# Row-wise infinity norm on one core: joined reductions in the tail's whole loads, and the first tile's store issued at the end

## Chip, core and metric

The kernel runs on one core of a Trainium2 chip. The metric is the device time of one execution in microseconds, given as the median of several runs. The core has several engines that run side by side and meet through semaphores: here VectorE (DVE) computes, SyncE (SP) issues the loads and the last store, ScalarE (ACT) issues the other two stores, and GpSimd (POOL) closes the program. Transfers between the chip's main memory (HBM) and the on-chip memory (SBUF, 128 partitions) are carried by 16 DMA engines.

## What is computed

```python
def setup_inputs():
    rows = 8192
    cols = 8192
    return {"x": np.random.randn(rows, cols).astype(np.float32)}

def reference(x: np.ndarray) -> np.ndarray:
    return np.linalg.norm(x, ord=np.inf, axis=1)
```

With `axis=1` this is the vector norm of each row: the largest absolute value of its 8192 numbers. 268 MB go in and 32 KB come out.

## The kernel before

Each of the 128 partitions handles 64 rows, in three groups with a result tile each: 2 rows of the first tile (`r_first`), 38 rows of the bulk (`r_bulk`) and 24 rows of the tail (`r_tail`). The input is loaded into one SBUF buffer, `ring`, which has room for three loads of two rows (`W` = 16384 columns) and a little padding.

The first loop (lines 263 to 268) does `N` = 20 loads of two rows for each partition, going round the three slots of the ring. Each load is followed by one reduction with two results: VectorE reads 128x16384 as two rows and writes 128x2. The first of these loads gives `r_first`, the other 19 give `r_bulk`. The reduction is `absmax` (line 254), so all of VectorE's instructions have line 255 in the profile.

The tail (lines 271 to 318) covers the last 24 rows of each partition as one line of 196608 columns, cut into the 37 loads of the list `TAIL`. Its first three entries are whole loads of 16384 columns that begin at a row's start; the later ones shrink from 15488 columns to 512, so that little work is left when the last one lands. A load that crosses a row's end is cut into pieces, one for each row. A piece that does not end its row gives a partial result, which is written into `ring` just in front of the place where the row's last piece will lie; the row's last piece is reduced together with these partial results, and gives the row's value in `r_tail`. The pieces of a load are separate VectorE instructions with one result each, in the whole loads too: each of these three gives two instructions of 128x8192, for two rows.

The places of the tail's loads in the ring follow from a small planner (lines 282 to 293): each load is put behind the one before it, rounded up to 128 columns with room for its partial results, and at the start of the ring again where it would run over the end. A load may only be written to where earlier reductions have read their data, so SyncE's issue of a load waits for VectorE. The tile framework makes these waits out of the reads and writes of the program; it also gives each DMA one of eight semaphores in turn, in the order of the DMAs in its schedule, and a DMA that gets a semaphore waits for the one that had it before, where that isn't implied already. Instructions of one engine run in the order in which they are issued.

The results leave in three stores. `r_bulk`'s and `r_first`'s are issued on ScalarE (lines 315 and 317), `r_tail`'s on SyncE (line 318). `r_bulk`'s has an explicit order behind the reduction of the third load from the end (`done`, line 316). `r_first`'s has none: it waits only for the first tile's reduction, and in ScalarE's program it stands ahead of `r_bulk`'s store.

Four passes work on the finished program. `drop_implied_waits` (line 134) takes out waits that other waits imply. `start_first_load_early` (line 34) puts the first load ahead of the opening barrier. `finish_on_pool` (line 71) lets GpSimd close the program alone: after the closing barrier it waits for the stores that nothing has waited for yet, clears the semaphores except the one of the last store (`r_tail`'s), and then waits for that one. `open_without_vector` (line 184) keeps VectorE out of the opening barrier.

Of the kernel before, what the change touches and what calls it, by code (L numbers as in the profile page):

```python
# [210 lines left out]
@with_exitstack  # L211
def kernel(
    ctx: ExitStack,
    tc: tile.TileContext,
    x: bass.AP,
    out: bass.AP,
    B: int = 2,
    SLOTS: int = 3,
    PAD: int = 128,
):  # L220
    nc = tc.nc
    P = nc.NUM_PARTITIONS
    rows, cols = x.shape
    W = B * cols
    R = SLOTS * W + PAD * 4


    n_tail = sum(w for _, w in TAIL) // cols
    met = 0
    for lo, w in sorted(TAIL):  # L230
        assert lo == met
        met += w
    assert met == n_tail * cols
    n_bulk_rows = rows // P - n_tail
    assert n_bulk_rows % B == 0
    N = n_bulk_rows // B
    split = n_bulk_rows * P
    x_f = x[: P * B].rearrange("(p b) c -> p (b c)", p=P)
    out_f = out[: P * B].rearrange("(p b) -> p b", p=P)
    x_b = x[P * B : split].rearrange("(p n b) c -> n p (b c)", p=P, b=B)  # L240
    out_b = out[P * B : split].rearrange("(p n) -> p n", p=P)
    x_t = x[split:].rearrange("(p t) c -> p (t c)", p=P)
    out_t = out[split:].rearrange("(p t) -> p t", p=P)

    pool = ctx.enter_context(tc.tile_pool(name="sbuf", bufs=1))
    r_first = pool.tile([P, B], F32)
    r_bulk = pool.tile([P, n_bulk_rows - B], F32)
    r_tail = pool.tile([P, n_tail], F32)
    used = [HEAD, B, n_bulk_rows - B, n_tail]
    gap = -sum(-(-n // STEP) * STEP for n in used) % PAD  # L250
    pool.tile([P, gap], F32, name="gap")
    ring = pool.tile([P, R], F32)

    def absmax(o, i):
        return nc.vector.reduce_max(  # L255
            out=o, in_=i, axis=X, apply_absolute_value=True
        )

    def after(ins, first, kind):
        info = mybir.DependencyInfo(kind, mybir.DependencyReason.SCHED_ONLY)  # L260
        tc.add_manual_dep(ins.ins, first.ins.name, info, reason="order")

    for n in range(N):
        at = n % SLOTS * W
        t = ring[:, at : at + W]
        nc.sync.dma_start(out=t, in_=x_f if n == 0 else x_b[n - 1])
        r = r_first[:] if n == 0 else r_bulk[:, (n - 1) * B : n * B]
        absmax(r, t.rearrange("p (b c) -> p b c", b=B))


    pieces = []
    for j, (at, w) in enumerate(TAIL):
        end = at + w
        while at < end:
            r = at // cols
            to = min(end, (r + 1) * cols)
            pieces.append((j, r, to - at))
            at = to
    of_row = [[k for k, s in enumerate(pieces) if s[1] == r] for r in range(n_tail)]


    here = N % SLOTS * W
    start, slot = [], []
    for j, (_, w) in enumerate(TAIL):
        first = next(s for s in pieces if s[0] == j)
        ks = of_row[first[1]]
        n_part = len(ks) - 1 if pieces[ks[-1]][0] == j else 0
        at = -(-(here + n_part) // PAD) * PAD
        if at + w > R:
            at = -(-n_part // PAD) * PAD  # L290
        start.append(at)
        slot.append(at - n_part)
        here = at + w

    for j, (src, w) in enumerate(TAIL):
        at = start[j]
        nc.sync.dma_start(out=ring[:, at : at + w], in_=x_t[:, src : src + w])
        here = [k for k, s in enumerate(pieces) if s[0] == j]
        offs = [at + sum(pieces[i][2] for i in here[:m]) for m in range(len(here))]
        todo = list(zip(here, offs))  # L300
        if slot[j] != at:

            todo = todo[1:] + todo[:1]
        for k, lo in todo:
            _, r, n = pieces[k]
            ks = of_row[r]
            if k == ks[-1]:
                frm = slot[j] if len(ks) > 1 else lo
                done = absmax(r_tail[:, r : r + 1], ring[:, frm : lo + n])
            else:  # L310
                to = slot[pieces[ks[-1]][0]] + ks.index(k)
                done = absmax(ring[:, to : to + 1], ring[:, lo : lo + n])
        if j == len(TAIL) - 3:

            ins = nc.scalar.dma_start(out=out_b, in_=r_bulk[:])
            after(ins, done, mybir.DependencyClass.Sync)
            nc.scalar.dma_start(out=out_f, in_=r_first[:])
    nc.sync.dma_start(out=out_t, in_=r_tail[:])
    nc.at_finalize(drop_implied_waits)
    nc.at_finalize(start_first_load_early)  # L320
    nc.at_finalize(finish_on_pool)
    nc.at_finalize(open_without_vector)
# [30 lines left out]
```

## Time and profile before

| what | value |
|---|---|
| median of 3 runs | 626.75 us (626.57 to 626.91) |
| the profiled execution | 626.98 us |
| its span (first to last instruction recorded) | 624.33 us |
| time outside the span | 2.65 us |
| one load of two rows, issue to landing | 40.7 us (median of 23) |
| `r_first`'s store, issue to landing | 23.5 us |
| `r_bulk`'s store, issue to landing | 1.5 us |
| `r_tail`'s store, issue to landing | 1.4 us |

How to read it: the page gives each engine's busy time and share of the span, then the DMA queues with packets, megabytes and share of 16 engines' time. In the rows of the timeline stand start and duration in us, the engine (with a q for its DMA issues), the line, the operation, the tile written and the tile read, their shapes, and how many instructions were merged; in brackets the engine's idle time just before, and what ended it. In the list of waits stand who waited, for whom, the us in total, the number of times and the longest. In the rows of groups stand the busy us and the mean ns of one, then the idle time before them. Consecutive VectorE instructions overlap a little in the records (by about 0.08 us), so durations do not add up exactly to distances between starts.

### The profile page before, as it was taken

Reading aid. Unit: us, or ns where it says so; the run is one execution under the profiler, and the core shown is the slowest. Engines: PE = TensorE matmul, PEld = TensorE weight load, DVE = VectorE, ACT = ScalarE, POOL = GpSimd, SP = SyncE. Lnnn points to the kernel's source line nnn. Section 1 sums busy time; section 2 is a strip of 40 time slices with the busy share of each in tenths; the row PEclk is TensorE's granted clock in tenths of the full one; section 3 lists DMA queues with packets and bytes.
Section 4 is the critical chain, followed back from the end, with each engine's and each line's share of the span. In section 5 each row is a group of like instructions: output and inputs, shape, how many; then the busy total and the mean of one; then the engine's idle time right before and its main releaser. Section 6 shows DMA issues by size and latency. Waiting matters only on the chain.

```text
span 624.3 us, 168 instructions
## 1 busy us (share of the span) xinstructions
DVE 553.2 (89%) x76; POOL 0.2 (0%) x4
## 2 busy tenths in 40 slices
DVE  0588988889988889888898888988899999999999
POOL 0000000000000000000000000000000000000000
DMA  9999999999999999999999999999999999999998
GB/s 403 470 403 458 416 428 445 403 470 403 470 403 470 403 466 407 458 416 428 445 403 470 403 470 403 470 403 470 392 435 458 408 446 427 421 437 424 431 425 335
DMA packets 8497, 268.47 MB, mean 430 GB/s; under 512 B 1200, under 2 KB 1200, under 8 KB 3120
## 3 DMA queue, kind: packets, MB, share of 16 engines
q1 hardware_dynamic: 8208, 268.44, 99.6%
q10 hardware_dynamic: 288, 0.02, 0.0%
q14 instruction: 1, 0.01, 0.0%
HBM read 268.44 MB, written 0.03 MB: 430 GB/s over the span
## 4 chain that ended last, share of the span: by engine, by line
DMA 61%; DVE 38%; issue 0%; DVEq 0%
DMA ring<-in_x_dram 61%; DVE r_bulk L255 17%; DVE ring L255 10%; DVE r_tail L255 9%; DVE r_first L255 3%; DVEq L348 0%
## 5 line engine op out<-in xcount | busy, mean ns | idle before, releaser
L255 DVE TENSOR_REDUCE r_bulk<-ring 128x2 f32<-128x16384 f32 x19 | 327.2, 17220 | 40.0 <-DMA ring<-in_x_dram 40.0
L255 DVE TENSOR_REDUCE r_tail<-ring 128x1 f32<-128x8192 f32 (+14 forms) x24 | 109.6, 4585 | 7.7 <-DMA ring<-in_x_dram 7.7
L255 DVE TENSOR_REDUCE ring<-ring 128x1 f32<-128x5248 f32 (+26 forms) x32 | 101.4, 3213 | 0.8 <-DMA ring<-in_x_dram 0.8
L255 DVE TENSOR_REDUCE r_first<-ring 128x2 f32<-128x16384 f32 x1 | 17.2, 17219 | 21.9 <-DMA ring<-in_x_dram 21.9
L337 POOL MEMSET const-bfloat16-1.0<- 128x1 bf16 x1 | 0.1, 101 | 0.0
L337 POOL MEMSET const-uint8-127<- 128x1 uint8 x1 | 0.1, 101 | 0.0
L337 POOL MEMSET const-float32-0.0<- 128x1 f32 x1 | 0.1, 98 | 0.2 <-issue 0.2
L337 POOL MEMSET const-float32-1.0<- 128x1 f32 x1 | 0.1, 98 | 0.0
## 6 DMA issues: line engine op xcount, KB each, us to landing
ring<-in_x_dram SPq DMA_DIRECT2D x1, 7744.0 KB, 39.6
ring<-in_x_dram SPq DMA_DIRECT2D x1, 7168.0 KB, 37.2
ring<-in_x_dram SPq DMA_DIRECT2D x1, 6400.0 KB, 32.9
ring<-in_x_dram SPq DMA_DIRECT2D x1, 5696.0 KB, 36.7
ring<-in_x_dram SPq DMA_DIRECT2D x1, 5056.0 KB, 41.0
ring<-in_x_dram SPq DMA_DIRECT2D x1, 4544.0 KB, 36.0
ring<-in_x_dram SPq DMA_DIRECT2D x1, 4032.0 KB, 32.0
ring<-in_x_dram SPq DMA_DIRECT2D x1, 3648.0 KB, 40.3
```

Of the source, the lines that this page charges most:

```text
L255: return nc.vector.reduce_max(out=o, in_=i, axis=X, apply_absolute_value=True)
L337: nc = _bacc.Bacc("TRN2", target_bir_lowering=False, num_devices=1)
```

## The change

The three whole loads of the tail get one reduction each, with two results, in the form that the bulk uses; they leave the loop body before the cutting into pieces. `r_first`'s store gets the same explicit order as `r_bulk`'s, behind the reduction of the third load from the end, and so stands behind `r_bulk`'s store in ScalarE's program.

```diff
     for j, (src, w) in enumerate(TAIL):
         at = start[j]
         nc.sync.dma_start(out=ring[:, at : at + w], in_=x_t[:, src : src + w])
+        if w == W and src % cols == 0:
+            r = src // cols
+            absmax(
+                r_tail[:, r : r + B],
+                ring[:, at : at + w].rearrange("p (b c) -> p b c", b=B),
+            )
+            continue
         here = [k for k, s in enumerate(pieces) if s[0] == j]
...
             ins = nc.scalar.dma_start(out=out_b, in_=r_bulk[:])
             after(ins, done, mybir.DependencyClass.Sync)
-            nc.scalar.dma_start(out=out_f, in_=r_first[:])
+            ins = nc.scalar.dma_start(out=out_f, in_=r_first[:])
+            after(ins, done, mybir.DependencyClass.Sync)
     nc.sync.dma_start(out=out_t, in_=r_tail[:])
```

In the built program VectorE has 73 reductions instead of 76. The eight DMA semaphores are handed out in another order, since `r_first`'s store no longer takes the third turn; each load still follows the load eight places before it on its semaphore. SyncE has one separate semaphore wait fewer (it stood at the ninth bulk load, for `r_first`'s store), and GpSimd has one more, for `r_first`'s store, ahead of its clearing of semaphores.

## The prediction

> **What bounds the kernel now.** I read the page from its DMA part first, since the kernel reads 268 MB and does one reduction on it.
>
> ```profile
> span 624.3 us, 168 instructions
> DVE 553.2 (89%) x76; POOL 0.2 (0%) x4
> q1 hardware_dynamic: 8208, 268.44, 99.6%
> q10 hardware_dynamic: 288, 0.02, 0.0%
> q14 instruction: 1, 0.01, 0.0%
> ```
>
> q1 is SyncE's queue, the loads: it keeps the 16 DMA engines busy for 99.6% of the span. VectorE works 89% of it. So the loads set the pace, and VectorE has slack, unless it lies in the wrong place. q10 is ScalarE's queue, which carries two of the three stores; q14 carried one packet of instructions. Both matter below. Next, who waited for whom:
>
> ```profile
> DVE r_bulk L255 <- DMA ring<-in_x_dram: 40.0, 19, 2.2
> DVE r_tail L255 <- DMA ring<-in_x_dram: 7.7, 5, 2.1
> DVE ring L255 <- DMA ring<-in_x_dram: 0.8, 1, 0.8
> ```
>
> VectorE waits some 2.1 us for every load of the bulk (40.0/19), in the tail five times (7.7 in all), and once more for 0.8 us. The timeline says where:
>
> ```profile
> 406.32 58.35 SPq L297 DMA_DIRECT2D ring<-in_x_dram  x4
> 408.36 17.28 DVE L255 TENSOR_REDUCE r_tail<-ring 128x1 f32<-128x8192 f32 x2 [2.07 <-DMA ring<-in_x_dram]
> 427.66 17.28 DVE L255 TENSOR_REDUCE r_tail<-ring 128x1 f32<-128x8192 f32 x2 [2.02 <-DMA ring<-in_x_dram]
> 447.04 17.28 DVE L255 TENSOR_REDUCE r_tail<-ring 128x1 f32<-128x8192 f32 x2 [2.10 <-DMA ring<-in_x_dram]
> 465.29 8.69 DVE L255 TENSOR_REDUCE r_tail<-ring 128x1 f32<-128x8192 f32 x1 [0.98 <-DMA ring<-in_x_dram]
> ...
> 573.24 0.33 SPq L297 DMA_DIRECT2D ring<-in_x_dram  x1
> 573.25 5.62 DVE L255 TENSOR_REDUCE ring<-ring 128x1 f32<-128x5248 f32 x1 [0.80 <-DMA ring<-in_x_dram]
> ```
>
> The three pairs are the instructions that the change joins; before and behind each VectorE waits for data. The last wait ends at 573.25; from there to 623.56 VectorE never waits. But it is not far behind the data: the semaphore events of the trace say that each later load lands 0.11 to 0.25 us before VectorE starts on it (0.024 us is the distance where it does wait). So the end is set by two things that run side by side with 0.1 to 0.2 us between them.
>
> **Part 1: one instruction instead of two, three times.** A pair takes 17.28 us from first start to last end. The joined form stands in the bulk, same shape:
>
> ```profile
> L255 DVE TENSOR_REDUCE r_bulk<-ring 128x2 f32<-128x16384 f32 x19 | 327.2, 17220 | 40.0 <-DMA ring<-in_x_dram 40.0
> ```
>
> 17.22 us, so 0.06 saved each, 0.18 in all. Behind the three pairs stand waits of 2.02, 2.10 and 0.98 us for data, so VectorE only waits 0.06 longer. What could pass on is the release of the slots: SyncE issues the next load just after the second half is done (425.64 to 425.67, 444.94 to 444.97, 464.31 to 464.34), and would now do so 0.06 earlier. A load lands 40.7 us after issue and takes 19.3 of DMA time, so about two are always queued ahead; an issue 0.06 earlier lands nothing earlier. The danger is the other sign: a load that needs only the first half of a slot could start after the first instruction today and would have to wait 8.6 us longer. I laid the ring out by the planner's rule: loads 3 and 4 of the tail (counted from 0) cover both halves of loads 0 and 1, and load 5 covers the end of load 1 and both halves of load 2. No load is freed by a first half alone. Bounds: -0.18 (no cover at all) to 0; I take 0.
>
> **Part 2: the early store goes.** Its 128 pieces of 8 bytes run between load packets from 42.8 to 62.4 us.
>
> ```profile
> 39.16 0.38 ACTq L317 DMA_DIRECT2D out_dram<-r_first  x1
> 41.21 17.22 DVE L255 TENSOR_REDUCE r_bulk<-ring 128x2 f32<-128x16384 f32 x1 [2.08 <-DMA ring<-in_x_dram]
> 60.65 17.22 DVE L255 TENSOR_REDUCE r_bulk<-ring 128x2 f32<-128x16384 f32 x1 [2.22 <-DMA ring<-in_x_dram]
> ```
>
> The wait grows from 2.08 to 2.22 there. A single interval varies anyway (19.27 to 19.38 elsewhere, in a pattern of four loads), so I compare four loads: 77.34 us from 41.21 to 118.55, against 77.30, 77.28 and 77.28 for the next three fours. The store cost the loads 0.04 to 0.06 us; by its packets, 9 for each engine at 9 ns, it would be 0.08. I take 0.06 saved. It passes to the end, because every later landing moves, the one at 573.2 included. Bounds: 0.04 to 0.08.
>
> **Part 3: the same store at the end.**
>
> ```profile
> 622.28 1.28 DVE L255 TENSOR_REDUCE r_tail<-ring 128x1 f32<-128x519 f32 x2
> 622.39 0.34 ACTq L315 DMA_DIRECT2D out_dram<-r_bulk  x1
> 623.59 0.35 SPq L318 DMA_DIRECT2D out_dram<-r_tail  x1
> ```
>
> ScalarE issues r_bulk's store at 622.39; its packets run from 623.24 to 623.47 and it lands at 623.85, 1.45 after issue. r_first's is queued right behind: issue at about 622.75, packets from 623.6 to about 623.8, landing at about 624.2. Its other waits (a landed load, the same reduction) are over by then. ScalarE would reach the closing barrier at about 623.3 instead of 622.9; SyncE reaches it at 624.1, so that is covered. r_tail's store is issued at 623.59, has packets from 624.4 and lands at 625.03: behind r_first's, and not beside it. GpSimd, which ends the program, leaves the barrier at 624.24 and waits for the ScalarE stores, clears semaphores, then waits for r_tail's. It gets one more wait, some 0.08 us (its barrier steps stand at 624.15 and 624.22), under the 0.8 us until 625.03. ScalarE's first DMA took 379 ns to issue and the second 338, so r_bulk's may be 0.04 late; hidden too. I take 0. Upper bound: if the two ScalarE stores ran strictly one behind the other, r_first's would land at 623.85 + 1.45 = 625.30, 0.27 behind the store that now ends last, and GpSimd's clearing, which now has 0.79 us of cover (624.24 to 625.03), would come after it: 0.27 + 0.79 + 0.08 = +1.14. Lower bound 0.
>
> The Trainium skill (DMA: Bandwidth & Descriptors, Anatomy of one DMA) gives a fixed cost of about 2.0 us for a DMA, most of it the receipt from memory. It is stated for another queue; by it r_first's store would land at 624.75, after the barrier, and if all of that counted the end would be 0.5 us later. The trace shows 1.45 for the neighbouring store.
>
> **Part 4: the instruction packet.** The page's one q14 packet is 8192 bytes, and lies at 570.37 to 570.68 us. The load that VectorE waits for at 573.25 took 7.16 us after the one before it, for 5248 columns, while 16384 columns take 19.31, so 6.19 for this one: 0.97 late. Until then the 16 parts of a load land within 0.5 us of each other; from then to the end within 1.3 to 1.4. So one DMA engine fell some 0.9 us behind and never caught up, and the end waits for it. I read it as an engine's program being fetched on as it runs. VectorE started its 48th reduction at 568.97, SyncE issued its last load before that at 566.13; 1.4 us from VectorE's step fits the 0.8 to 1.0 us from issue to first packet of other DMAs better. With three instructions fewer VectorE reaches that place in its program at 583.2, three reductions on; SyncE (one separate semaphore wait fewer) would reach it at 573.2. Either way the engine still falls behind, only later: VectorE starts the load of 573.25 up to 0.80 earlier, gets ahead, and then waits for the late engine. What is gained at the end is the smallest distance left between landing and start: 0.111 - 0.024 = 0.09 us if the packet falls before the next load lands (578.7), 0.163 - 0.024 = 0.14 if at 585. I take 0.12. Bounds: 0 (it doesn't move) to 0.80 (it no longer hurts).
>
> The Trainium skill (Runtime: NRT & Kernel Launch, Instruction fetch mechanics) says that crossing a block boundary of the program is mostly hidden. By that rule this part gives nothing, and the sum would be 626.7; here the engine that carried the packet was late by 0.97 us on the row that ended VectorE's wait.
>
> **Sum.** 0 - 0.06 + 0 - 0.12 = -0.18 us. The profiled execution took 626.98 (span 624.33 and 2.65 around it), so it would take 626.80. It was 0.23 above the median of 626.75, to which I apply the same difference: 626.57, say 626.6.
>
> **Rivals.** *The late engine is spared*: the packet moves to where it costs nothing. For: an engine that is ahead could carry it, as parts land 0.5 us apart. Against: lag has stayed for 50 us, and VectorE's program must still be read. Price: the 0.80 wait and the 0.06, so 625.9. *The closing store decides (slower)*: r_first's store lands late and GpSimd starts its clearing after it. Place: GpSimd after 624.24; it decides when the landing comes after that by more than the slack under 625.03, which the trace doesn't show. For: my landing of 624.2 is almost at the barrier. Against: packets of 9 to 14 ns, and both earlier stores landed within 1.5 us. Price 0.08 to 1.14 less 0.06, the middle 627.3. *Only the early store counts*: the packet doesn't move, or not with these instructions: 626.7.
>
> **Chances.** Forecast 0.50, only the early store 0.20, late engine spared 0.12, closing store 0.15, something unseen 0.03. The range 625.8 to 627.2 holds the first three and half of the fourth, about 9 in 10 by these cases; I leave it there because the bounds of parts 3 and 4 reach these ends. The likeliest case's own range is 626.4 to 626.75. By 0.2%, or 1.25 us, which is about what a measurement of this kernel can tell from no change, none of the priced cases differs. What is left outside are errors of my reading: a larger lag moved by the packet on the one side, the closing sequence on the other: faster 0.07, same 0.87, slower 0.06.
>
> **What would show it.** Part 1: waits of about 2.1 and 1.0 behind three reductions of 17.22. Part 2: no larger wait at 60.6. Part 3: two ScalarE issues after 622, landing before r_tail's store. Part 4: the 0.80 at 573 gone, a wait of up to 0.9 some loads later, and q14's packet near it. It is wrong if VectorE waits longer than before at any load before 573, if the DMA rate of the bulk changes, or if the time around the span is no longer 2.65.

## The result, and the profile after

The changed kernel takes 628.18 us (median of 16 runs, 627.75 to 628.72) against 626.87 for the kernel before (16 runs, 626.57 to 627.47): a ratio of 1.0019, 95% interval 1.0012 to 1.0026. It is 1.31 us slower, where 0.2 us faster was forecast. The profiled execution took 628.36 us.

The page first, its header and the rows of engines and of SyncE's queue:

```profile
span 624.3 us, 164 instructions
DVE 553.0 (89%) x73; POOL 0.2 (0%) x4
q1 hardware_dynamic: 8208, 268.44, 99.7%
```

The span is what it was, 624.3 us. So the loss lies outside the span: 628.36 - 624.31 = 4.05 us here, 2.65 before. Over the 16 runs the time outside is 4.1 us (median), and the span's median 624.0; for the kernel before, 33 later runs give 2.64 and 624.2. The change took about 0.2 us off the span and added 1.47 behind it.

What happens behind the span is seen in the DMA records. The timeline of the end, then the stores' rows in the table of DMA issues (queue, number, size, us from issue to last landing):

```profile
622.27 1.28 DVE L255 TENSOR_REDUCE r_tail<-ring 128x1 f32<-128x519 f32 x2
622.38 0.37 ACTq L322 DMA_DIRECT2D out_dram<-r_bulk  x1
622.79 0.44 ACTq L324 DMA_DIRECT2D out_dram<-r_first  x1
623.58 0.35 SPq L326 DMA_DIRECT2D out_dram<-r_tail  x1
```

```profile
out_dram<-r_bulk ACTq DMA_DIRECT2D x1, 19.0 KB, 1.7
out_dram<-r_first ACTq DMA_DIRECT2D x1, 1.0 KB, 3.3
out_dram<-r_tail SPq DMA_DIRECT2D x1, 12.0 KB, 2.8
```

Before, the last of these rows read:

```profile
out_dram<-r_tail SPq DMA_DIRECT2D x1, 12.0 KB, 1.4
```

The issues stand where they were expected. The smallest store, 1 KB, takes the longest: 3.3 us. The store behind it, `r_tail`'s, is issued at the same moment as before (623.58 against 623.59) and lands after 2.8 us where it took 1.4. The store ahead of it on the same queue, `r_bulk`'s, is a little late too: 1.7 us where it took 1.5. By the semaphore events the 16 parts of `r_first`'s store land between 624.14 and 626.05, one part after another, although all its packets had left by 623.94. Of `r_tail`'s 16 parts six land by 624.93, as before, and the other ten up to 626.41. Before, the last one landed at 625.03. The time of the execution is the last landing, counted from the span's start, plus 626.98 - 625.03 = 1.95 us before and 628.36 - 626.41 = 1.95 after (any time ahead of the span's start is in the 1.95): the later landing is the whole loss.

The joined reductions stand as forecast, with the same waits behind them:

```profile
408.77 17.22 DVE L255 TENSOR_REDUCE r_tail<-ring 128x2 f32<-128x16384 f32 x1 [2.09 <-DMA ring<-in_x_dram]
428.05 17.22 DVE L255 TENSOR_REDUCE r_tail<-ring 128x2 f32<-128x16384 f32 x1 [2.06 <-DMA ring<-in_x_dram]
447.37 17.22 DVE L255 TENSOR_REDUCE r_tail<-ring 128x2 f32<-128x16384 f32 x1 [2.10 <-DMA ring<-in_x_dram]
465.68 8.69 DVE L255 TENSOR_REDUCE r_tail<-ring 128x1 f32<-128x8192 f32 x1 [1.09 <-DMA ring<-in_x_dram]
```

And the instruction packet has moved from 570.37 to 581.72 us: in the window from 581 to 583 us the queue rows show it, and the timeline shows the wait of 0.80 us at 573 gone and one of 0.38 at 583.65:

```profile
572.75 10.07 DVE L255 TENSOR_REDUCE ring<-ring 128x1 f32<-128x5248 f32 x2
...
583.65 0.28 DVE L255 TENSOR_REDUCE ring<-ring 128x1 f32<-128x128 f32 x1 [0.38 <-DMA ring<-in_x_dram]
```

```profile
q14 instruction: 1, 0.01, 1.0%
```

### The profile page after: what moved, and what is told of

Read it like the earlier page. It is cut to its first block, busy times and chain, and to the rows that moved or that the text cites. A ratio compares the mean times of both kernels' runs of the same rounds, so it can differ in the third digit from the quotient of the medians.

```text
span 624.3 us, 164 instructions
## 1 busy us (share of the span) xinstructions
DVE 553.0 (89%) x73; POOL 0.2 (0%) x4
## 4 chain that ended last, share of the span: by engine, by line
DMA 62%; DVE 38%; issue 0%; DVEq 0%
DMA ring<-in_x_dram 62%; DVE r_bulk L255 17%; DVE ring L255 9%; DVE r_tail L255 9%; DVE r_first L255 3%; DVEq L356 0%
## 5 line engine op out<-in xcount | busy, mean ns | idle before, releaser
L255 DVE TENSOR_REDUCE r_tail<-ring 128x2 f32<-128x16384 f32 (+15 forms) x21 | 109.4, 5218 | 7.9 <-DMA ring<-in_x_dram 7.9
```

The lines of the kernel that those rows point to most:

```text
L255: return nc.vector.reduce_max(out=o, in_=i, axis=X, apply_absolute_value=True)
```

## The experiments

In each, "outside" is the time of a run less its span. All diffs are against the changed kernel unless another is named; they show the lines that matter, and `...` marks what is left out. The time that a result is set against is the kernel before's, run beside it. Experiments 7 to 11 are single executions, without an interval.

**1. The joined reductions alone.**

```diff
-            ins = nc.scalar.dma_start(out=out_f, in_=r_first[:])
-            after(ins, done, mybir.DependencyClass.Sync)
+            nc.scalar.dma_start(out=out_f, in_=r_first[:])
```

> Only the joined reductions; r_first's store stays early. Theory A (the store at the end costs the time: its 8-byte pieces are acknowledged late and hold back r_tail's landing): r_tail's store lands about 1.4 us after issue as before, the time outside the span is 2.65 us as before, and the time is 0 to 0.3 us under the kernel before (the instruction packet moves from 570 to about 582 us and the wait of 0.80 us shrinks). Rival B (the joined reductions cost the time, by some wait at the end that the records don't show): 1.1 to 1.4 us above the kernel before, about 628.2.

Measured: 626.85 us (11 runs) against 626.90, ratio 0.9995 (0.9987 to 1.0004), outside 2.64 for both. `r_tail`'s store lands 1.4 us after issue, with the same row as in the kernel before. The joined reductions cost nothing at the end.

**2. The moved store alone** (against the kernel before).

```diff
-            nc.scalar.dma_start(out=out_f, in_=r_first[:])
+            ins = nc.scalar.dma_start(out=out_f, in_=r_first[:])
+            after(ins, done, mybir.DependencyClass.Sync)
```

> Only the store is moved; VectorE keeps 76 reductions. Theory A: r_first's store lands more than 3 us after issue, r_tail's about 2.8 us after issue, the time is 1.2 to 1.6 us above the kernel before. Rival B: no slower than the kernel before. Beside it, for the instruction packet: if VectorE's place in its program sets it off, it stays at 570.4 us with the wait of about 0.8 us at 573; if SyncE's does (one separate wait fewer), it moves to 574 to 578 us.

Measured: 628.11 us (11 runs) against 626.90, ratio 1.0019 (1.0010 to 1.0028), outside 4.07 (median).

```profile
out_dram<-r_first ACTq DMA_DIRECT2D x1, 1.0 KB, 2.8
out_dram<-r_tail SPq DMA_DIRECT2D x1, 12.0 KB, 2.5
```

That is a little under what was written for them. `r_bulk`'s store, ahead of them, took 1.9 us. The store alone makes the whole loss. This kernel also says who sets off the instruction packet. The timeline, and the queue rows of the window from 569.5 to 571.5 us:

```profile
573.20 5.62 DVE L255 TENSOR_REDUCE ring<-ring 128x1 f32<-128x5248 f32 x1 [0.61 <-DMA ring<-in_x_dram]
```

```profile
q14 instruction: 1, 0.01, 1.0%
```

With 76 reductions and SyncE's shorter program it stays at 570.3 us, while in the first experiment, with 73 reductions and SyncE's program as before, it stands at 581.75. It goes with VectorE's program. In all fourteen traces it comes 3.4 to 4.2 us after VectorE starts its 47th reduction, whichever reduction that is.

**3. No store of `r_first` at all.**

```diff
...
-    x_b = x[P * B : split].rearrange("(p n b) c -> n p (b c)", p=P, b=B)
-    out_b = out[P * B : split].rearrange("(p n) -> p n", p=P)
+    x_b = x[:split].rearrange("(p n b) c -> n p (b c)", p=P, b=B)
+    out_b = out[:split].rearrange("(p n) -> p n", p=P)
...
-            ins = nc.scalar.dma_start(out=out_f, in_=r_first[:])
-            after(ins, done, mybir.DependencyClass.Sync)
```

> The first tile's rows become part of the bulk, 40 rows for each partition, and their results leave with r_bulk's store in pieces of 160 bytes; there is no store of r_first at all. Joined reductions as in the changed kernel. Theory A: r_tail's store lands about 1.4 us after issue, 2.65 us outside the span, time 0.1 to 0.4 us under the kernel before, so about 626.6. Rival C (what costs is that ScalarE's queue has no early DMA any more, or that the semaphores are handed out in another order): about 628, like the changed kernel. The rows of a load lie 40 rows apart in memory here and not 38, which could change the loads' rate; the landings of the bulk tell (19.3 us for each).

Measured: 626.61 us (11 runs) against 626.90, ratio 0.9996 (0.9987 to 1.0005), outside 2.64, loads of the bulk 19.3 us each. ScalarE's queue has no early DMA here, and the loads' semaphores go round as in the changed kernel: neither shows a cost.

**4. The same small pieces, spread out.** The loads are those of the third experiment, and `r_first` keeps its own store at the end.

```diff
...
+    out_all = out[:split].rearrange("(p n) -> p n", p=P)
+    out_f, out_b = out_all[:, :B], out_all[:, B:]
...
```

> Both stores at the end as in the changed kernel, but the first tile's two rows are the first of each partition's 40, so that r_first's 128 pieces of 8 bytes go to places 160 bytes apart and not to one stretch of 1 KB. Theory A1 (many small pieces into the same few memory lines are written one after another): r_first's store lands within 1.7 us, r_tail's after about 1.4, the time is that of the kernel with one store, about 626.7. Theory A2 (a piece of 8 bytes costs some 15 ns at the memory wherever it goes): r_first's lands 3.3 us after issue as in the changed kernel, and the time is about 628.2.

Measured: 626.51 us (11 runs) against 626.90, ratio 0.9995 (0.9986 to 1.0004), outside 2.64. The stores' rows:

```profile
out_dram<-r_bulk ACTq DMA_DIRECT2D x1, 19.0 KB, 1.5
out_dram<-r_first ACTq DMA_DIRECT2D x1, 1.0 KB, 1.5
out_dram<-r_tail SPq DMA_DIRECT2D x1, 12.0 KB, 1.4
```

The same 128 pieces of 8 bytes, at the same place in the program, from the same queue: 1.5 us. It is not the small piece, but where its neighbours lie.

**5. The moved store some 12 us earlier, while loads still run.**

```diff
+        if j == len(TAIL) - 14:
+            ins = nc.scalar.dma_start(out=out_f, in_=r_first[:])
+            after(ins, done, mybir.DependencyClass.Sync)
         if j == len(TAIL) - 3:
...
-            ins = nc.scalar.dma_start(out=out_f, in_=r_first[:])
-            after(ins, done, mybir.DependencyClass.Sync)
```

> The changed kernel, but r_first's store is ordered behind the reduction of the 14th load from the end, so it is issued at about 610.7 us, some 12 us ahead of r_tail's store; where it goes is as in the changed kernel. Theory A (pieces of 8 bytes into one KB are taken slowly, and what is stored right behind them waits): 2.64 us outside the span as in the kernel before, time 626.5 to 626.9. Rival (any store of r_first that is late in ScalarE's program costs the time): 628.1.

Measured: 628.28 us (11 runs) against 627.06, ratio 1.0015 (1.0007 to 1.0024), outside 2.68, but the span's median is 625.6 where the kernel before has 624.4. I was right on what lies outside and wrong on the time; the rival's 628.1 comes close, but its loss lies inside the span. The timeline around the store, and SyncE's waits after 600 us:

```profile
610.33 0.38 ACTq L321 DMA_DIRECT2D out_dram<-r_first  x1
615.72 1.35 DVE L255 TENSOR_REDUCE ring<-ring 128x1 f32<-128x1152 f32 x1 [0.85 <-DMA ring<-in_x_dram]
617.34 3.07 DVE L255 TENSOR_REDUCE ring<-ring 128x1 f32<-128x1024 f32 x3 [0.27 <-DMA ring<-in_x_dram]
```

```profile
SPq L297 <- DMA out_dram<-r_first: 5.5, 1, 5.5
```

The pieces leave between 613.8 and 615.2, and the two loads that land around them come late: VectorE waits 0.85 and 0.27 us where the changed kernel shows no wait, together 1.1 us, about the loss. What leaves beside or behind the slow pieces comes late, loads as well as stores. SyncE is also held for 5.5 us, since a load has to wait for the store whose semaphore it takes over; the loads were late before that wait ended at 617.6.

**6. The two ScalarE stores in the other order.**

> The changed kernel with the two ScalarE stores in the other order, r_first's ahead of r_bulk's, both behind the same reduction. Theory A: r_first's store starts 0.4 us earlier, so r_tail's lands some 0.4 us earlier than in the changed kernel, and the time outside the span falls from 4.1 to about 3.7; r_bulk's store, now behind it, lands over 2 us after issue where it took 1.5 to 1.7. Time about 627.8.

Measured: 628.60 us (8 runs) against 627.06, ratio 1.0024 (1.0014 to 1.0035), outside 4.59: a miss, and it got worse than the changed kernel, not better.

```profile
out_dram<-r_bulk ACTq DMA_DIRECT2D x1, 19.0 KB, 3.7
out_dram<-r_first ACTq DMA_DIRECT2D x1, 1.0 KB, 3.1
out_dram<-r_tail SPq DMA_DIRECT2D x1, 12.0 KB, 3.4
```

`r_first`'s store begins 0.4 us earlier, as written, and its last part lands 0.5 us earlier. But `r_bulk`'s, now behind it, is slowed to 3.7 us and passes that on: `r_tail`'s last part lands at 627.04. The expectation had left out that a held-up store holds up the next.

**7 and 8. Pieces 32 and 64 bytes apart.** The first 4 (8) loads cover 8 (16) rows of each partition; results of the first two rows leave at the end, the others early.

```diff
...
+    out_g = out[: P * G].rearrange("(p g) -> p g", p=P)
+    out_f, out_s = out_g[:, :B], out_g[:, B:]
...
```

> As the changed kernel, but the first 4 loads cover 8 rows of each partition that lie together; results of the first two rows are stored at the end in pieces of 8 bytes 32 bytes apart (a stretch of 4 KB), those of the other six early. How late r_first's store lands (3.3 us after issue when the pieces lie side by side, 1.5 when 160 bytes apart) tells what the pieces share: if it is a line of 64 bytes or less, two pieces share one here and the landing comes under 2.0 us after issue; if it is a stretch of some hundred bytes or more, it stays between 2.0 and 3.0.

> The same with 8 loads and 16 rows of each partition: pieces of 8 bytes 64 bytes apart (a stretch of 8 KB). Shared line of 64 bytes or less: lands 1.4 to 1.6 us after issue, as with 160 bytes. A wider shared stretch: still over 1.7.

Measured, one execution each: `r_first`'s store lands 1.5 us after issue in both, outside 2.7 in both. Already 32 bytes apart nothing is left of the delay. The kernel with 64 bytes took 626.90 us; the one with 32 took 644.81, because its fifth to seventh loads came 22 to 24 us apart and not 19.3, and the bulk's later ones 19.3 to 20.8. Why, I did not find. The fifth load is the first that reads rows in steps of 32 rows, exactly 1 MiB, from partition to partition (24, 36, 38 or 40 rows in the other kernels); that this is the cause is not shown. The end of that execution is otherwise like the others.

**9. The store in two halves of 4-byte pieces.**

```diff
-            ins = nc.scalar.dma_start(out=out_f, in_=r_first[:])
-            after(ins, done, mybir.DependencyClass.Sync)
+            for k in range(B):
+                ins = nc.scalar.dma_start(
+                    out=out_f[:, k : k + 1], in_=r_first[:, k : k + 1]
+                )
+                after(ins, done, mybir.DependencyClass.Sync)
```

> The changed kernel with r_first's store cut in two, first all of its first results and then all of its second ones: 256 pieces of 4 bytes, 8 bytes apart, in place of 128 of 8, into the same KB. If each piece costs its 15 ns in turn, whatever its size, the last landing comes some 1.9 us later than in the changed kernel, the time outside the span grows from 4.1 to about 6, time about 630. If the cost goes by bytes or by the stretch of memory, it stays at about 4.1.

Measured, one execution: 631.92 us, span 624.1.

```profile
out_dram<-r_tail SPq DMA_DIRECT2D x1, 12.0 KB, 6.5
```

The first half's last part lands at 625.78, the second half's at 629.69, `r_tail`'s at 629.87. The same 1 KB in twice the pieces costs 3.5 us more than in the changed kernel, where I had written 1.9. The first half's 128 pieces of 4 bytes take (625.78 - 623.95)/128 = 14 ns each, the changed kernel's 128 pieces of 8 bytes (626.05 - 624.14)/128 = 15 ns: the number of pieces counts, not their bytes. Those that come second into the same places cost about twice as much here: 629.69 - 625.78 = 3.9 us for 128, some 30 ns each.

**10 and 11. Pieces 16 bytes apart, and pieces of 16 bytes side by side.** The tenth is the eighth with 4 rows in the group. In the eleventh all 4 rows' results leave together.

> As with the pieces 32 bytes apart, which landed without delay, but 16 bytes apart (the first two loads cover 4 rows of each partition; a stretch of 2 KB). If pieces that share 32 bytes of memory are taken one after another, two share them here and the landing is late: over 1.8 us after issue. If a line of 64 bytes is what is shared, 32 bytes apart should already have been late, so no delay here would leave only full adjacency as the cause.

> The first two loads, 4 rows of each partition, form the first group, and their results are stored at the end in 128 pieces of 16 bytes side by side (2 KB). If it is the smallness against a shared 32 bytes that costs, these pieces are late as well, between 1.8 and 3.3 us after issue, and the time outside the span is between 2.7 and 4.1; if only pieces of 8 bytes suffer, 1.5 and 2.64.

Measured, one execution each: 626.86 and 626.60 us. The kernel before took 626.95 beside them, one execution too. The rows of `r_first`'s store, of the tenth and of the eleventh:

```profile
out_dram<-r_first ACTq DMA_DIRECT2D x1, 1.0 KB, 1.5
```

```profile
out_dram<-r_first ACTq DMA_DIRECT2D x1, 2.0 KB, 1.5
```

Neither is late. Both of my readings (32 bytes shared, small pieces in general) fall, and so does adjacency by itself, since the eleventh's pieces lie side by side: one piece for each 16 bytes is free, two are not.

**12. Every other piece.** The tenth and eleventh also spread over 2 KB and not 1, so a stretch of 1 KB that takes one piece at a time was still open.

```diff
+    nc.scalar.dma_start(out=out_f[1:P:2], in_=r_first[1:P:2, :])
...
-            ins = nc.scalar.dma_start(out=out_f, in_=r_first[:])
+            ins = nc.scalar.dma_start(out=out_f[0:P:2], in_=r_first[0:P:2, :])
             after(ins, done, mybir.DependencyClass.Sync)
```

> The changed kernel, but r_first's results from the odd partitions are stored early, after the bulk's loads are issued, and only those from the even ones at the end: 64 pieces of 8 bytes, 16 bytes apart, in the same one KB as in the changed kernel. If pieces that lie in the same 16 bytes hold each other up, no two do here: r_first's last store lands 1.5 us after issue, 2.64 us outside the span, time about 626.8. If it is the stretch of one KB that takes one piece after another at 15 ns, 64 of them land about 1 us late (2.4 us after issue), the time outside the span is about 3.1 to 3.6.

Measured: 626.73 us (8 runs) against 626.80, ratio 0.9998 (0.9986 to 1.0009). The store at the end is issued at 622.84, its packets leave from 623.98 to 624.16, some 0.2 us later than in the changed kernel, and it lands between 624.34 and 624.51. That is 1.7 us after issue where 1.5 was written, but only 0.35 us behind its last packet, as in the tenth (0.38). `r_tail`'s lands after 1.5 us. In the same 1 KB, 64 pieces of 8 bytes that don't share 16 bytes are not held up at all, where 15 ns for each would have made 0.96 us.

## Why the prediction was wrong

**Part 1 (joined reductions, 0)** was right: 17.22 us each, waits of 2.06, 2.10 and 1.09 behind them where there were 2.02, 2.10 and 0.98, and without the moved store (experiment 1) the ratio is 0.9995 with an interval that holds 1.

**Part 2 (early store gone, -0.06)** isn't borne out. The first four intervals of the bulk sum to 77.34 us with the early store (kernel before and experiment 1) and to between 77.30 and 77.42 without it (changed kernel, experiments 2 to 6, 9 and 11). What I took for its cost is the scatter of these sums. Its value is below what these sums can show. The store's pieces also ended at 60.2 and not at 62.4; what the trace has after that are 4-byte packets.

**Part 3 (the store at the end, 0)** is the step that failed. The issue times, the packets (623.73 to 623.94, some 0.1 us later than written) and the barrier were as I had them; the landing was not. I took 1.45 us from `r_bulk`'s store, the row next to it on the same queue, and ended the store's cost with its packets. The packets' own 7 to 9 ns do not show when their pieces land: the landings came over 1.9 us, 15 ns for each piece (1.5 us, 11 ns, in experiment 2's trace), and ten of the sixteen parts of `r_tail`'s store came late with them. My upper bound, two stores one after the other, was 1.14 and so still too low; the measured term is the time outside, 4.11 - 2.64 = 1.47 us. Of the signs I named, the last came: the time around the span is no longer 2.65. The trace did hold a hint: the only store in pieces of 8 bytes was the one I was moving, and where it had been it was thinned out, mostly sixteen pieces every 2.4 us, from 42.8 to 60.2 us. I had no row for these pieces sent all at once, and took the nearest store for it although its pieces were nineteen times as large.

The Trainium skill (DMA: Bandwidth & Descriptors, Specifications) says that transfers under 512 bytes are done as read-modify-write. By that rule alone all three stores here, in pieces of 152, 8 and 96 bytes, would be treated alike. The runs show pieces of 8 bytes 16 bytes apart and of 16 bytes side by side landing in 1.5 us, so the rule doesn't tell this store from the others.

**Part 4 (the instruction packet, -0.12)** was right that the packet goes with VectorE's program: it moved from 570.4 to 581.7 us with three instructions fewer, the 0.80 us wait went, and a wait came back later. It was not right on the step: I put it 1.4 us behind the start of the 48th reduction, and in the changed kernel it lies 1.0 us ahead of that start (582.73). A distance from the 47th fits all traces (experiment 2); which step of VectorE's program it is stays open. The size isn't shown. The median span fell by about 0.2 us between the two kernels, against 0.18 forecast for parts 2 and 4 together, but single spans scatter from 623.7 to 624.8, and experiment 1, where the packet moved as far, has the median of the kernel before, 624.2 (its mean is 0.2 lower).

**The rivals.** The closing store was the right suspect for the slower side, with the wrong mechanism: GpSimd's clearing decides nothing in the changed kernel. In thirteen of the fourteen kernels profiled the time is the last landing plus 1.94 to 1.96 us, however late `r_first`'s store is. The other is experiment 9, with 2.06: there `r_first`'s last part lands only 0.18 us ahead of `r_tail`'s (0.36 in the changed kernel). A clearing of about 0.28 us, an estimate from these two figures (0.18 + 0.10), would explain it; my upper bound had 0.79 for it. So neither the point from which it decides nor its price could come out right, and the range ended a microsecond too low.

**What stays open.** Why two pieces in one stretch of 16 bytes hold each other up. Sharing alone isn't enough: `r_bulk`'s pieces of 152 bytes also meet inside 16 bytes at every second border, and land in 1.5 us. Nor do the runs tell shared 16 bytes from crowding over a longer stretch: every late layout of `r_first`'s results has two pieces in each 16 bytes, all others at most one, and no run has pairs of neighbours with gaps between the pairs. That late pieces hold their DMA engine, and through it `r_tail`'s parts and the loads of experiment 5, fits the landings; which engine carried which part is not in the records I read.

## What to carry to other kernels

Before a store is moved to where nothing covers it, look at its pieces and not at its bytes: 128 neighbouring pieces of 8 bytes cost 1.5 us at the end of the program and nothing measurable when load packets spread them over 17 us. Give each partition's results one longer piece: 40 rows in one store, which also takes a store away, ran at 626.61 us, and pieces of 16 bytes at 626.60 in one execution. That takes the loss away; a gain over the kernel before is not shown, since an interval (experiment 3) holds 1 and the other has none. And for the end of a program, add up to the last landing and not to the last issue: here the time was the last landing plus 1.95 us.

## What the runs showed that was not expected

- Pieces of 8 bytes side by side, sent within 0.2 us, landed over 1.9 us; the same pieces 16, 32, 64 or 160 bytes apart landed 1.5 us after issue (1.7 for the 64 pieces of experiment 12).
- DMAs beside one whose pieces are held up come late on either queue: behind it `r_tail`'s store, 2.8 us and not 1.4, and `r_bulk`'s, 3.7 and not 1.5 (experiment 6); just ahead of it `r_bulk`'s, 1.7 (1.9 in experiment 2); beside it two loads, for which VectorE waited 0.85 and 0.27 us (experiment 5).
- One instruction packet of 8 KB, 0.31 us long, left its mark on the loads to the end: after it the 16 parts of a load land within 1.0 to 1.4 us and not 0.5.
